# Loading a 2 KB-wide strip of the first tile in three transfers (112, 8 and 8 rows) instead of one of 128 rows

## The chip, the cores and the metric

The kernel runs on one core of one Trainium2 chip. The metric is device time in microseconds (us) per execution; the kernel before takes 121.96 us, the median of three runs that lie between 121.9 and 121.97. All other times in this document are from one profiled execution, and are counted from the first instruction in its span.

## The reference

The input is 32 x 3 images of 256 x 256 float32, 25.17 MB. Each image is turned by 180 degrees:

```python
def reference(x):                                   # x: (32, 3, 256, 256) float32
    return np.rot90(x, k=2, axes=(-2, -1)).astype(np.float32)
```

Turning an image by 180 degrees reverses the order of its 65,536 numbers. No arithmetic is done on them: the work is 25.17 MB read from device memory (HBM), 25.17 MB written back, and a reversal between the two.

## The kernel before

The 96 images are taken in three groups of 32. An image is cut in four parts of 16,384 numbers, and a group then has 32 x 4 = 128 rows of 16,384 numbers (64 KB), one for each partition of the on-chip memory. Three tiles, `A`, `Bt` and `Ct`, hold the three groups; all three fit at the same time, so no tile is used twice and nothing waits for a buffer to come free. A small tile `T` of 2,048 columns is scratch.

For a group there are three steps:

1. *Load* (`load`, line 49): the 128 rows are copied from `x` into the tile. The loads of `Bt` and `Ct` are one transfer each, issued by the SP engine's queue. The load of `A` is two transfers: columns 512 to 16,383 through SP (line 62), and the strip of columns 0 to 511, 2 KB of each row, through the queue of the ACT engine (line 63). ACT has no other work in this kernel.
2. *Turn* (`turn` and `swap`, lines 54 to 71): VectorE (DVE) reverses every row in place. A piece of width `w` is swapped with the piece at the mirrored place in three copies: the high end reversed into `T`, the low end reversed to the high end, and `T` to the low end. All three are recorded at line 44. `A` and `Ct` are turned in four pieces of 2,048 columns (12 copies), `Bt` in six pieces of up to 1,366 (18 copies).
3. *Store* (`store`, line 52): the tile is written to `out`, the four parts of each image in reverse order. All three stores go through SP's queue.

The order on each queue follows the program text. SP issues: load `A` (columns from 512), load `Bt`, load `Ct`, store `A`, store `Bt`, store `Ct`. DVE does all of `A`, then all of `Bt`, then all of `Ct`, in program order, because `copy` asks for that order. Two waits matter below. The first copy of `A` (`T<-A`) reads the last 2,048 columns of the tile, so it waits for SP's transfer alone; the second (`A<-A`) reads columns 0 to 2,047, which hold the strip, so it is the one that waits for ACT's transfer. And the store of `A` has a manual dependency (lines 75 to 79) on the last copy of `Bt`: SP doesn't issue the first store before DVE has turned both `A` and `Bt`, and the two stores behind it on SP wait with it.

Of the kernel before, what the change touches and what calls it, by code (L numbers as in the profile page):

```python
# [2 lines left out]

os.environ.setdefault("NEURON_RT_ULTRASERVER_MODE", "4")

# [4 lines left out]


@with_exitstack
def kernel(
    ctx: ExitStack,
    tc: tile.TileContext,
    x: bass.AP,
    out: bass.AP,
):
    nc = tc.nc  # L20
    P = 128

    B, C, H, W = x.shape
    L = H * W
    G = 32
    E = L // 4
    J = E // 8

    x4 = x.rearrange("b c h w -> (b c) (h w)").rearrange(
        "(g n) (s e) -> g (n s) e", n=G, s=4)  # L30
    o4 = out.rearrange("b c h w -> (b c) (h w)").rearrange(
        "(g n) (s e) -> g n s e", n=G, s=4)

    pool = ctx.enter_context(tc.tile_pool(name="slots", bufs=1))
    A = pool.tile([P, E], x.dtype, tag="A")
    Bt = pool.tile([P, E], x.dtype, tag="B")
    Ct = pool.tile([P, E], x.dtype, tag="C")
    T = pool.tile([P, J], x.dtype, tag="T")

    def back(t, lo, hi):  # L40
        return t[:, hi - 1:(lo - 1 if lo else None):-1]

    def copy(dst, src):
        c = nc.vector.tensor_copy(out=dst, in_=src)  # L44
        tc.keep_in_program_order(c)
        return c

    def load(t, g, lo=0, hi=E, queue=nc.sync):
        return queue.dma_start(out=t[:, lo:hi], in_=x4[g][:, lo:hi])  # L49

    def store(t, g):
        return nc.sync.dma_start(out=o4[g][:, ::-1, :], in_=t[:, :])

    def swap(t, lo, w):
        hi = E - lo - w
        copy(T[:, 0:w], back(t, hi, hi + w))
        copy(t[:, hi:hi + w], back(t, lo, lo + w))
        return copy(t[:, lo:lo + w], T[:, 0:w])

    half = E // 2  # L60

    load(A, 0, 512, E)
    load(A, 0, 0, 512, nc.scalar)
    load(Bt, 1)
    load(Ct, 2)

    def turn(t, pieces):
        step = -(-half // pieces)
        for lo in range(0, half, step):
            last = swap(t, lo, min(step, half - lo))  # L70
        return last

    turn(A, 4)
    last = turn(Bt, 6)
    tc.add_manual_dep(
        store(A, 0).ins, last.ins.name,
        mybir.DependencyInfo(
            mybir.DependencyClass.Sync, mybir.DependencyReason.DATA),
        reason="the first store goes when the loads are nearly done")
    store(Bt, 1)  # L80
    turn(Ct, 4)
    store(Ct, 2)


# [1 line left out]
_INS = ['x']  # L86
_OUTS = [((32, 3, 256, 256), 'float32')]


# [23 lines left out]
```

## Time and profile before

| What | us |
|---|---|
| median of the three timed runs | 121.96 |
| span of the profiled execution (first to last instruction) | 120.1 |
| DVE busy | 45.2, in 42 copies |
| one DVE copy of 2,048 / 1,366 columns | 1.23 / 0.87 |
| SP's load of `A`, issue to landing | 21.9 |
| ACT's strip, issue to landing | 22.1 |
| load of `Bt` / of `Ct`, issue to landing | 40.8 / 59.7 |
| store of `A` / of `Bt` / of `Ct`, issue to landing | 22.2 / 40.9 / 42.7 |

The page gives no time for the profiled execution except its span; the timed runs lie 1.9 us above that span. A transfer's time to landing counts from its issue and includes its time behind earlier transfers in the same queue. Bytes are moved by 16 DMA engines; a transfer's rows are dealt out to them. In the trace each record of a DMA engine is called a packet. Here a packet is one row of one transfer, or the 4-byte write with which a DMA engine reports on a semaphore that its share of a transfer is done. SP's queue is q1 in the records, ACT's is q10.

### The profile page before, as it was taken

The numbers are of one execution on the slowest core, as the hardware profiler recorded it, in microseconds if no ns is written. First come the engines' busy times: TensorE is split into PE (matmuls) and PEld (weight loads), VectorE is DVE, ScalarE is ACT, GpSimd is POOL, SyncE is SP. The second block draws the span as 40 slices with busy tenths as digits, with TensorE's granted clock in tenths as the row PEclk, the third lists the DMA queues.
The fourth block names the chain that finished last, engine by engine and source line by source line (L and its number), as shares of the span: only waits on it lengthen the run. The fifth ranks groups of instructions, "written<-read, shape, count | busy, mean of one in ns | idle before, by whom it ended". The sixth has DMA issues, their size and how long they took to land.

```text
span 120.1 us, 99 instructions
## 1 busy us (share of the span) xinstructions
DVE 45.2 (38%) x42; POOL 0.2 (0%) x4
## 2 busy tenths in 40 slices
DVE  0000000499995099999459999400000000000000
POOL 0000000000000000000000000000000000000000
DMA  9888988899889988998899889988898889888980
GB/s 338 349 349 349 699 349 349 360 633 415 349 349 589 459 349 349 568 480 349 349 502 546 349 349 458 589 349 349 349 699 349 349 349 699 349 349 349 677 371 0
DMA packets 1008, 50.33 MB, mean 419 GB/s; under 512 B 112, under 2 KB 112, under 8 KB 240
## 3 DMA queue, kind: packets, MB, share of 16 engines
q1 hardware_dynamic: 864, 50.07, 96.9%
q10 hardware_dynamic: 144, 0.26, 0.6%
HBM read 25.17 MB, written 25.17 MB: 419 GB/s over the span
## 4 chain that ended last, share of the span: by engine, by line
DMA 34%; DVE 26%; another core or an unknown queue 2%; issue 1%; SPq 0%; DVEq 0%
DMA Bt<-in_x_dram 34%; DVE Bt L44 9%; DVE T L44 9%; DVE Ct L44 8%; SPq L49 0%; DVEq L44 0%
## 5 line engine op out<-in xcount | busy, mean ns | idle before, releaser
L44 DVE COPY T<-A 128x2048 f32<-128x2048 f32 x4 | 4.9, 1227 | 22.8 <-DMA A<-in_x_dram 22.7
L44 DVE COPY T<-Bt 128x1366 f32<-128x1366 f32 (+1 forms) x6 | 5.2, 873 | 4.5 <-DMA Bt<-in_x_dram 4.3
L44 DVE COPY T<-Ct 128x2048 f32<-128x2048 f32 x4 | 4.9, 1227 | 3.2 <-DMA Ct<-in_x_dram 3.1
L44 DVE COPY Bt<-T 128x1366 f32<-128x1366 f32 (+1 forms) x6 | 5.2, 873 | 0.2
L44 DVE COPY Bt<-Bt 128x1366 f32<-128x1366 f32 (+1 forms) x6 | 5.2, 872 | 0.2
L44 DVE COPY Ct<-T 128x2048 f32<-128x2048 f32 x4 | 4.9, 1227 | 0.1
L44 DVE COPY A<-T 128x2048 f32<-128x2048 f32 x4 | 4.9, 1227 | 0.1
L44 DVE COPY Ct<-Ct 128x2048 f32<-128x2048 f32 x4 | 4.9, 1227 | 0.1
L44 DVE COPY A<-A 128x2048 f32<-128x2048 f32 x4 | 4.9, 1226 | 0.1
L97 POOL MEMSET const-bfloat16-1.0<- 128x1 bf16 x1 | 0.1, 102 | 0.0
L97 POOL MEMSET const-uint8-127<- 128x1 uint8 x1 | 0.1, 102 | 0.0
L97 POOL MEMSET const-float32-0.0<- 128x1 f32 x1 | 0.1, 98 | 0.2 <-issue 0.2
L97 POOL MEMSET const-float32-1.0<- 128x1 f32 x1 | 0.1, 98 | 0.0
## 6 DMA issues: line engine op xcount, KB each, us to landing
A<-in_x_dram SPq DMA_DIRECT2D x1, 7936.0 KB, 21.9
A<-in_x_dram ACTq DMA_DIRECT2D x1, 256.0 KB, 22.1
Bt<-in_x_dram SPq DMA_DIRECT2D x1, 40.8
Ct<-in_x_dram SPq DMA_DIRECT2D x1, 59.7
out_dram<-A SPq DMA_DIRECT2D x1, 22.2
out_dram<-Bt SPq DMA_DIRECT2D x1, 40.9
out_dram<-Ct SPq DMA_DIRECT2D x1, 42.7
```

The source lines that it names most:

```text
L44: c = nc.vector.tensor_copy(out=dst, in_=src)
L97: nc = _bacc.Bacc("TRN2", target_bir_lowering=False, num_devices=1)
```

## The change

The strip of `A` is still loaded through ACT's queue, and every element goes where it went. The one transfer of 128 rows becomes three transfers: rows 0 to 111, rows 112 to 119, rows 120 to 127. ACT issues them one after the other. Each has its own semaphore, so the second copy of `A` (`A<-A`), which waited for one strip transfer, waits for three; so does the store of `A`, which in the kernel before lists the strip's semaphore among its waits too. Everything else, the order on SP's queue and on DVE included, is as it was.

```diff
     load(A, 0, 512, E)
-    load(A, 0, 0, 512, nc.scalar)
+    for r0, r1 in ((0, 112), (112, 120), (120, 128)):
+        nc.scalar.dma_start(out=A[r0:r1, 0:512], in_=x4[0][r0:r1, 0:512])
     load(Bt, 1)
     load(Ct, 2)
```

## The prediction, made before the changed kernel ran

> **What bounds the kernel now.** I read the page's DMA part first, because DVE is busy for only 38% of the span.
>
> ```profile
> DMA  9888988899889988998899889988898889888980
> ...
> q1 hardware_dynamic: 864, 50.07, 96.9%
> q10 hardware_dynamic: 144, 0.26, 0.6%
> ...
> A<-in_x_dram SPq DMA_DIRECT2D x1, 7936.0 KB, 21.9
> A<-in_x_dram ACTq DMA_DIRECT2D x1, 256.0 KB, 22.1
> ```
>
> The DMA engines are busy from start to end: 96.9% + 0.6% of all 16. The kernel is bound by bytes, and its time changes only if a DMA engine gets more to do or falls idle. The last two lines show something else: 256 KB through ACT took as long as 7,936 KB through SP. The packet records tell why. They carry no engine number, but each begins within some nanoseconds of another's end, so they fall into 16 chains, one for each DMA engine. This is the chain whose eighth row of `A` ends last (start us, queue, bytes, ns):
>
> ```
> 17.393 q1  63488 2342
> 19.732 q10  2048   84
> 19.812 q1  63488 2342
> 22.150 q10  2048   84
> 22.230 q1      4    9
> 22.236 q10     4    9
> 22.242 q1  65536 2418
> 24.656 q1  65536 2418
> ```
>
> A DMA engine takes the two queues in turn, one packet from each: a row from SP, a strip row from ACT, and so on. The 4-byte completion writes take turns too (SP's stood between the last strip row and the strip's own). So a strip row costs 0.08 us of the DMA engine but waits one SP row, 2.34 to 2.42 us, for its turn. Eight strip rows beside eight rows of `A` finish together, at 22.2.
>
> Next the timeline, to see what stands between the loads and the stores:
>
> ```profile
> 0.73 0.38 ACTq L49 DMA_DIRECT2D A<-in_x_dram  x1
> 0.73 0.39 SPq L49 DMA_DIRECT2D A<-in_x_dram  x1
> ...
> 22.69 1.23 DVE L44 COPY T<-A 128x2048 f32<-128x2048 f32 x1 [22.69 <-DMA A<-in_x_dram]
> 23.95 1.23 DVE L44 COPY A<-A 128x2048 f32<-128x2048 f32 x1
> ...
> 36.56 1.23 DVE L44 COPY A<-T 128x2048 f32<-128x2048 f32 x1
> 42.11 0.87 DVE L44 COPY T<-Bt 128x1366 f32<-128x1366 f32 x1 [4.32 <-DMA Bt<-in_x_dram]
> ...
> 57.53 0.87 DVE L44 COPY Bt<-T 128x1362 f32<-128x1362 f32 x1
> 58.43 0.63 SPq L52 DMA_DIRECT2D out_dram<-A  x1
> 59.10 0.59 SPq L52 DMA_DIRECT2D out_dram<-Bt  x1
> 61.45 1.23 DVE L44 COPY T<-Ct 128x2048 f32<-128x2048 f32 x1 [3.05 <-DMA Ct<-in_x_dram]
> ```
>
> `A` is turned by 37.79, then DVE waits 4.32 us for `Bt`; `Bt` is turned by 58.40, and SP issues the first store at once. The waits of SP confirm that the store waited for DVE and nothing else at the end:
>
> ```profile
> SPq L52 <- DVE Bt L44: 35.5, 1, 35.5
> ```
>
> By the packet records the rows of `Ct`'s load end at 60.46 to 60.88 on the 16 DMA engines, and each takes its first store row 2 to 5 ns later. The store was issued 2.0 to 2.4 us ahead. That lead, and the 4.32 us before `Bt`, is all the slack DVE has.
>
> **The change part by part.**
>
> *More issues on ACT.* Two further issues of about 0.38 us (the row at 0.73) put the last at about 1.6 us. ACT has nothing else to do, and the strip rows are first needed at 21.8: nothing, bounded by 0 and by the 20 us of that cover.
>
> *Bytes per DMA engine.* 128 rows were 8 on each chain. 112 rows over 16 are 7 each; the two transfers of 8 rows have no example in the trace. I take one row each on eight DMA engines (the shown transfers deal equal numbers of whole rows); the other end, all eight rows on one DMA engine, is a rival below. If both use the same eight, these get 9 strip rows and 3 completion writes: +0.08 + 2 x 0.006 = +0.09 us; the others get 7: -0.08 us. The DMA engine that ends last sets the end, and which group it is in isn't recorded: -0.08 to +0.09, I take 0. On that spread the Trainium skill ("DMA: Bandwidth & Descriptors", section "Why a DMA increments its semaphore by 16 and not by 1") says that a transfer uses the largest number up to 16 that divides its rows, the lowest-numbered DMA engines first, so 8 and the same 8; no run here shows it yet.
>
> *Turns.* On a DMA engine of the eight, ACT's queue now holds seven rows, completion 1, a row, completion 2, a row, completion 3: 12 packets instead of 9. Played on the chain above, with SP's eighth row of `A` ending at t: completion 1, SP's own completion, second strip row, a row of `Bt` (2.41), completion 2, a row of `Bt` (2.41), third strip row, a row of `Bt` (2.41), completion 3. That is t + 3 x 2.414 + 2 x 0.08 + 2 x 0.006 = t + 7.42. t is 21.71 to 22.15 on the 16 chains, at least 21.90 for the latest of any eight, so the last completion is at 29.32 to 29.57. From record to landing it is 0.42 (SP's load of `A`) to 0.62 (the strip: 22.24 to 22.86): 29.74 to 30.2. I take 30.1, since the strip's own row is the nearest.
>
> *The second copy.* `A<-A` starts at 30.1 instead of 23.95. Behind it on DVE stand ten more copies of `A`, 13.84 us to 37.79 before. They now end at 43.94 and eat the 4.32 us of waiting: `Bt`'s first copy starts at 43.97, not 42.11, 1.86 us later (1.5 to 1.95 by the range above). Its 18 copies take the same 16.29 us, so SP issues the first store at 60.29 (59.93 to 60.38) instead of 58.43. `Ct` lands at 61.36, so its turn isn't late. The store of `Bt`, queued behind on SP, is hidden by the 19 us of `A`'s rows.
>
> *The gap between loads and stores.* The only transfer in the trace that meets idle DMA engines is the first load: issued at 0.73, first packets at 1.756 to 2.086 (1.03 to 1.36 later), ends of these at 4.777 to 5.222, so 3.0 to 3.4 us for what later takes 2.34. The store then begins at 60.29 + 1.03 to 1.36 = 61.32 to 61.65 on DMA engines that are idle since 60.4 to 60.9. Their first store rows ended at 63.30 at the latest. Without any cold start, the last now ends at 61.65 + 2.42 = 64.07: +0.77. With the load's cold start, 60.29 + 4.49 + 0.08 = 64.86: +1.56, or +1.80 if the store's longer issue (0.63 beside 0.39) counts as well. The 23 rows behind it run as before, so this is the change of the end. I take +1.25, about midway: a store reads on-chip memory, and the cold row is a load's. With the early and late ends of the issue the bounds are +0.4 and +1.9.
>
> Sum: span 120.1 + 1.25 = 121.3; with the 1.9 us by which the timed median lies above the profiled span, 123.2 us.
>
> **The rivals.**
>
> *Hidden after all (not slower).* If fewer turns are needed, say because a completion write and the row behind it go in one turn, the strip lands one or two turns earlier, at 27.7 or 25.2. DVE's slip of 6.15 us becomes 3.7 or less and the 4.32 us before `Bt` cover it. The point that decides: the free slip is 42.11 - 37.82 = 4.29 us, and about 1.0 us more, since a store issued at 59.5 still reaches the DMA engines by 60.88. Landings up to 29.2 cost nothing; my figure is 0.5 to 1.0 beyond that. Time: 121.96 - 0.08 to + 0.09, so 121.9 to 122.05. Against it: every 4-byte write in the records took a turn of its own. The Trainium skill speaks for it ("DMA: Bandwidth & Descriptors", section "Queues, rings and completion order"): a DMA engine takes a whole packet from one queue, typically 9 to 17 descriptors, before it switches, by which ACT's remaining packets would go together and this rival would hold; the trace's strict alternation of single rows disagrees. Chance 0.14.
>
> *More turns.* The 8-row transfers lie on fewer DMA engines. On four, two rows each: two more turns, landing at 35.1, store issued 5 us later still, 128 us; on one, some 13 turns more, above 150. One turn more for a reason that I don't see: 125.7. Chance together 0.10.
>
> *Better balance (faster).* The DMA engines end at 118.45 to 118.94. If the late ones all lose a row and the strip stays hidden, -0.08 us; a gain above 0.24 needs a mechanism that no row shows. Chance 0.02.
>
> **How the numbers follow.** The forecast, a gap of 0.4 to 1.9 us (122.3 to 123.9), has 0.74, likeliest 123.2. The range takes in the hidden case below and a little above the forecast's own range: 121.9 to 124.1; it leaves out the more-turns case and tails. A measurement here tells 0.2%, 0.24 us, from no change. Slower by more: 0.70 of the forecast (a gap that just closes takes 0.04 from it) and 0.10, so 0.80; same 0.18 (the hidden case and those 0.04); faster 0.02.
>
> The Trainium skill advises against such splits altogether ("DMA: Bandwidth & Descriptors", section "Rules for kernel authors": one 128-partition transfer, since parts run on the same DMA engines); it names no price.
>
> **What would show it.** In the profile after: 160 packets in q10 (128 rows, 16 + 8 + 8 completions); the third strip transfer landing at about 30; idle time of some 6.1 us before the second copy of `A` with a DMA as its end; no wait before `Bt`; the first store issued near 60.3; a slice of lower DMA share near 61; each later landing about 1.2 us later. The prediction is wrong if `A<-A` starts before 29.2, if the store's rows begin less than 1 us after its issue, or if the strip lands near 35 or later.

## The result and the profile after

The changed kernel takes 123.47 us (median of four runs, 123.46 to 123.73) where the kernel before takes 121.94: a ratio of 1.0131 (95% interval 1.0117 to 1.0146), 1.5 us slower. The forecast was 123.2, in a range of 121.9 to 124.1.

These are the same parts of the page as before, now of the changed kernel: the DMA engines' busy tenths in 40 slices, the queues, and the DMA issues with their time to landing.

```profile
span 121.9 us, 103 instructions
...
DMA  9778998899778977897787977797779777977990
...
q1 hardware_dynamic: 864, 50.07, 96.2%
q10 hardware_dynamic: 160, 0.26, 0.6%
...
A<-in_x_dram SPq DMA_DIRECT2D x1, 7936.0 KB, 23.0
A<-in_x_dram ACTq DMA_DIRECT2D x1, 224.0 KB, 22.8
A<-in_x_dram ACTq DMA_DIRECT2D x2, 16.0 KB
...
Ct<-in_x_dram SPq DMA_DIRECT2D x1, 60.8
```

ACT's queue has 160 packets, 16 completions more than before. But two lines say something that was not foreseen: SP's load of `A` takes 23.0 us to land instead of 21.9, and that of `Ct` 60.8 instead of 59.7. The loads themselves became slower. Next the timeline of the changed kernel around the waits (start, duration, engine, line; in brackets the idle time before it and what ended it):

```profile
0.73 1.32 ACTq L64 DMA_DIRECT2D A<-in_x_dram  x3
...
23.74 1.23 DVE L44 COPY T<-A 128x2048 f32<-128x2048 f32 x1 [23.74 <-DMA A<-in_x_dram]
31.05 1.23 DVE L44 COPY A<-A 128x2048 f32<-128x2048 f32 x1 [6.08 <-DMA A<-in_x_dram]
...
43.66 1.23 DVE L44 COPY A<-T 128x2048 f32<-128x2048 f32 x1
44.92 0.87 DVE L44 COPY T<-Bt 128x1366 f32<-128x1366 f32 x1
...
61.24 0.62 SPq L52 DMA_DIRECT2D out_dram<-A  x1
...
62.52 1.23 DVE L44 COPY T<-Ct 128x2048 f32<-128x2048 f32 x1 [1.31 <-DMA Ct<-in_x_dram]
```

The new wait of 6.08 us stands before the second copy of `A`, the wait before `Bt` is gone, and the first store is issued at 61.24 instead of 58.43. A slice of lower DMA share near 61 us, which the forecast looked for, does not stand out in the DMA row, since the whole row is lower than before. The packet records give the gap: the last rows of `Ct` end at 61.40 to 61.92 on the 16 DMA engines, their first store rows begin together at 62.51 to 62.66. From the last end to the last beginning it is 0.74 us of idle time.

In this profile, of an execution that took 123.73 us, the end of the last store row is 1.87 us later than before (120.80 beside 118.93): 1.04 had accumulated when the last row of `Ct` ended (61.92 beside 60.88), and the rest arose at the gap and behind it. So the loss has two parts, of which one was not in the prediction's sum. The experiments separate them.

### The profile page after: what moved, and what is told of

It is laid out like the page before. It is cut to its first block, busy times and chain, and to the rows that moved or that the text cites. A ratio compares the mean times of both kernels' runs of the same rounds, so it can differ in the third digit from the quotient of the medians.

```text
span 121.9 us, 103 instructions
## 1 busy us (share of the span) xinstructions
DVE 45.2 (37%) x42; POOL 0.2 (0%) x4
## 4 chain that ended last, share of the span: by engine, by line
DVE 36%; DMA 24%; another core or an unknown queue 1%; issue 1%; ACTq 1%; DVEq 0%
DMA A<-in_x_dram 24%; DVE T L44 11%; DVE Bt L44 9%; DVE A L44 8%; DVE Ct L44 8%; ACTq L64 1%; DVEq L44 0%
## 6 DMA issues: line engine op xcount, KB each, us to landing
Ct<-in_x_dram SPq DMA_DIRECT2D x1, 60.8
```

## The experiments

Three theories stood against each other. *W*: the late strip makes DVE late, hence the first store, hence the DMA engines fall idle (the prediction's). *L*: three transfers slow the loads. *U*: the uneven shares (nine strip rows on eight DMA engines, seven on the others) are at fault. When L had proved right in part, it was split further, into *S* (each additional transfer or packet has a price) and *P* (a strip row slows others when a DMA engine writes it to partitions that another one is writing).

### The changed kernel once more

> The changed kernel once more, unaltered. In its first profile the end came 1.87 us later than before, of which 0.8 us arose at the gap between the last row of the load of Ct (61.92) and the first store rows (62.51 to 62.66), and 1.04 us earlier: rows of A between about 9 and 22 us took 2.42 to 2.66 us where before all took 2.34. Theory L (the three transfers themselves slow the loads): the slow rows are there again, A lands near 23.7, the time is 123.4 to 123.7. Theory C (chance of that execution): rows of A take 2.34 us again, A lands at 22.6 to 22.9, the first store is issued near 60.3 and the last landing is about 0.9 us later than before; a time of 122.9.

123.51 us, ratio 1.0134 (1.0118 to 1.015). `A` lands at 23.24 (0.73 + 22.5), between the figures of the two theories, `Ct` at 62.06 instead of 61.36, and the last store row ends 1.56 us later than before. The lateness of the loads is there again, 0.70 us; the additional 0.3 of the first profile was that execution's own. Theory C falls.

### Three even transfers: 96, 16 and 16 rows

```diff
-    for r0, r1 in ((0, 112), (112, 120), (120, 128)):
+    for r0, r1 in ((0, 96), (96, 112), (112, 128)):
```

> Also three strip transfers, but of 96, 16 and 16 rows, so that each DMA engine gets 8 strip rows (6, 1, 1) and 11 packets of ACT. Theory W (the late strip makes DVE, the first store and so the DMA engines wait): played by turns, the third completion goes after two rows of Bt instead of three, landing at 27.7; the slip of DVE is 3.7 us, the 4.3 us of waiting before Bt cover it, the first store goes at 58.4 and the time is 121.9 to 122.0. Theory N (three transfers cost as such, whatever DVE does): as the changed kernel, 123.4. If the loads alone are slowed by the number of transfers: 122.3 to 122.9.

122.89 us, ratio 1.0076 (1.0058 to 1.0094). The timeline of this variant:

```profile
29.05 1.23 DVE L44 COPY A<-A 128x2048 f32<-128x2048 f32 x1 [4.08 <-DMA A<-in_x_dram]
43.53 0.87 DVE L44 COPY T<-Bt 128x1366 f32<-128x1366 f32 x1 [0.64 <-DMA Bt<-in_x_dram]
59.85 0.63 SPq L52 DMA_DIRECT2D out_dram<-A  x1
62.89 1.23 DVE L44 COPY T<-Ct 128x2048 f32<-128x2048 f32 x1 [3.06 <-DMA Ct<-in_x_dram]
```

With two turns instead of three, DVE waits 4.08 us for the strip and still 0.64 for `Bt`: the slip is covered, as W has it, and the store rows follow those of `Ct` without a gap. The strip landed at 28.93, later than the 27.7 counted for it. Still 0.94 us are lost, where W alone had nothing, and with even shares: U doesn't explain it, L does.

### Four even transfers

```diff
-    for r0, r1 in ((0, 112), (112, 120), (120, 128)):
+    for r0, r1 in ((0, 80), (80, 96), (96, 112), (112, 128)):
```

> Four strip transfers, 80, 16, 16 and 16 rows: every DMA engine gets 8 strip rows (5, 1, 1, 1) and 12 packets of ACT, as many as the eight busier ones have in the changed kernel, but the bytes are even. Theory W: third-row turn as there, landing near 30.1, the first store near 60.3 or a little later with the loads, time 122.9 to 123.6, as the changed kernel. Theory U (the uneven shares, 9 strip rows on eight DMA engines and 7 on the others, make the loss): 121.9 to 122.0.

124.25 us, ratio 1.0174 (1.0153 to 1.0196). The last completion lands at 30.76 and the first store is issued at 61.08, with a gap behind the loads again. As many turns as in the changed kernel, and at least as large a loss without any imbalance: U is out. The time lies 0.65 above the range given; the profiled execution was the shortest of the five (123.64), so why the others take longer isn't seen.

### The strip used last

```diff
-    def turn(t, pieces):
+    def turn(t, pieces, inside_out=False):
         step = -(-half // pieces)
-        for lo in range(0, half, step):
+        los = list(range(0, half, step))
+        for lo in los[::-1] if inside_out else los:
...
-    turn(A, 4)
+    turn(A, 4, inside_out=True)
```

> The changed kernel with its three transfers as they are, but A is turned from the inside out: the piece that reads the strip comes fourth instead of first. Its A<-A then would start at about 35.3 and the strip, landing at 30 to 31, is not waited for. Theory W: no wait for the strip, A turned by 37.8 to 38.9, DVE waits for Bt again, the first store is issued 2 us ahead of the loads' end, no gap; 121.9 to 122.0 if the loads are not slowed by the three transfers, 122.3 to 123.0 if they are (theory L). If DVE's wait isn't the cause: 123.4.

122.63 us, ratio 1.0059 (1.0045 to 1.0074). The same three transfers, but nothing waits for them:

```profile
43.09 0.87 DVE L44 COPY T<-Bt 128x1366 f32<-128x1366 f32 x1 [4.43 <-DMA Bt<-in_x_dram]
59.42 0.63 SPq L52 DMA_DIRECT2D out_dram<-A  x1
```

The wait before `Bt` is back at 4.43 us and the gap is gone. It takes 0.88 us less than the changed kernel beside it, which is the price of the gap; 0.68 us remain, which is the price of the slower loads.

### No manual dependency

```diff
     turn(A, 4)
-    last = turn(Bt, 6)
-    tc.add_manual_dep(
-        store(A, 0).ins, last.ins.name,
...
+    store(A, 0)
+    turn(Bt, 6)
```

> The changed kernel without the manual dependency: the store of A is issued after A is turned (near 45), and lines up on SP's queue behind the load of Ct. The late strip remains, but no gap can arise. Theory L (three transfers slow the loads by 0.65 to 0.75 us, apart from the gap): as the variant turned from the inside out, 122.5 to 122.8. If that variant's 122.6 came from its other order of copies: 121.95 here.

122.69 us, ratio 1.0062 (1.0042 to 1.0082). The other way of closing the gap, with the store issued at 44.50 and DVE still waiting 6.04 us for the strip, gives the same. So the remaining loss doesn't depend on the order of the copies.

```profile
30.64 1.23 DVE L44 COPY A<-A 128x2048 f32<-128x2048 f32 x1 [6.04 <-DMA A<-in_x_dram]
```

### The gap alone

```diff
+    for _ in range(5):
+        copy(T[:, 0:J], back(A, E - J, E))
     turn(A, 4)
```

> The kernel before, with its one strip transfer, and five more copies of 2,048 columns into the scratch tile ahead of turning A (their result is overwritten; nothing else changes). That makes DVE late by 5 x 1.26 = 6.3 us without touching a transfer. Theory G (the gap between loads and stores has its price by itself, and the slower loads are a second, separate loss): rows of A take 2.34 us as before, A lands at 22.7, the first store is issued near 60.4, its rows begin about 1.3 us later, idle DMA engines for 0.7 to 1.0 us; time 122.7 to 122.95, that is 0.8 to 1.0 more than before and less than the changed kernel. If the gap explains all of the loss: 123.4. If a late store costs nothing: 121.95.

123.38 us, ratio 1.0122 (1.0107 to 1.0137). Here the transfers are those of the kernel before, and `Ct` lands at 61.38 as there; the store is issued late:

```profile
span 121.2 us, 104 instructions
...
22.71 7.53 DVE L44 COPY T<-A 128x2048 f32<-128x2048 f32 x6 [22.71 <-DMA A<-in_x_dram]
60.47 0.63 SPq L52 DMA_DIRECT2D out_dram<-A  x1
61.48 1.23 DVE L44 COPY T<-Ct 128x2048 f32<-128x2048 f32 x1 [1.03 <-DMA Ct<-in_x_dram]
```

The last row of `Ct` ends at 60.98 (0.10 later than before), the first store rows begin at 61.75 to 61.90 (0.92 from the last end to the last beginning), take 2.47 instead of 2.42 us, and the rows behind them lose another 0.1 in sum: the last store row ends 1.13 us later than before, and the span is 1.1 longer. This shows the gap as a cause by itself. The time, though, grew by 1.48, above the range given and equal to the 123.4 of the theory that the gap explains all of the loss. That theory is out by the two variants above, which lose 0.68 and 0.79 us without a gap. Of the 1.48, the span shows 1.1; 2.2 us lie outside the span in all four executions, where the kernel before, run beside it, and the other variants have 1.8. Where those 0.4 us come from stays open; the five additional instructions are the only other difference.

### Two transfers of all rows, half as wide

```diff
-    load(A, 0, 0, 512, nc.scalar)
+    load(A, 0, 0, 256, nc.scalar)
+    load(A, 0, 256, 512, nc.scalar)
```

together with the removal of the manual dependency as above, on the kernel before.

> The strip in two transfers of all 128 rows, 256 columns each, so that each DMA engine writes strip rows to the same partitions as its rows of A, as before; 18 packets of ACT on every DMA engine. They land late, near 44, so the store of A has no manual dependency here and everything DVE does stays covered. Theory P (strip rows slow the loads when a DMA engine writes them to partitions that another DMA engine is writing at full rate): rows of A take 2.34 us plus nothing, the time is 121.9 to 122.1. Theory S (more strip transfers or packets on ACT's queue slow the loads as such): slow rows of A and Bt, at least as many as with three transfers, 122.5 or more.

122.98 us, ratio 1.0085 (1.007 to 1.01), a time that speaks for S; but the trace does not. With 288 packets ACT's queue has more than in any other variant, and yet every row of `A` behind the first takes 2.342 us, every row of `Bt` 2.418 us, as before. All of the loss is in the last rows of `Ct`, which began at 58.14 to 58.59 and took 2.94 to 3.79 us instead of 2.42. The first store had been issued at 56.33, earlier than in the kernel before (58.43) and later than in the variant without the manual dependency (44.50):

```profile
56.33 0.63 SPq L52 DMA_DIRECT2D out_dram<-A  x1
```

That was tested apart, with `turn` returning the last copy of its first piece:

```diff
-    turn(A, 4)
-    store(A, 0)
-    turn(Bt, 6)
+    turn(A, 4)
+    first = turn(Bt, 6)
+    tc.add_manual_dep(
+        store(A, 0).ins, first.ins.name,
...
```

> The two transfers of 128 rows by 256 columns once more, with the first store issued near 59 (after the first piece of Bt) instead of at 56.3. In the first of the two all rows of A and of the loads up to 58 took their normal time, and the 0.86 us that were lost arose in the last rows of the load of Ct, beginning 1.8 us after the store was issued. If the time of the store's issue did that: no slow rows at all here, 121.9 to 122.1. If the strip transfers did it, whatever the store: the last rows of Ct slow again, 122.9 to 123.1.

121.99 us, ratio 1.0003 (0.9994 to 1.0013). The timeline shows the same late strip (18.80 us of waiting) and the store now issued at 58.93:

```profile
span 120.1 us, 102 instructions
...
42.34 1.23 DVE L44 COPY A<-A 128x2048 f32<-128x2048 f32 x1 [18.80 <-DMA A<-in_x_dram]
58.93 0.63 SPq L52 DMA_DIRECT2D out_dram<-A  x1
```

No slow rows of `Ct`, no loss. So the 0.86 us went with the moment of the store's issue, and 18 strip packets on each DMA engine cost nothing measurable: S falls. (Six of the 256 rows of `Bt` and `Ct` took 0.04 to 0.2 us more in this profile, and none but the last rows of `Ct` in the one before it; that stays unexplained.)

### Which rows go together: halves, and even and odd rows

Both variants have two transfers of 64 rows, 4 + 4 rows and two completions on each DMA engine. First the halves:

```diff
-    for r0, r1 in ((0, 112), (112, 120), (120, 128)):
+    for r0, r1 in ((0, 64), (64, 128)):
```

> The strip in two transfers of 64 rows (0 to 63, 64 to 127): 4 + 4 rows and two completions on every DMA engine, landing near 25.3, covered by DVE's slack. Theory P: rows land on other DMA engines than with one transfer of 128, so rows of A take more than 2.34 us by some 0.04 to 0.09 us each; if half of the rows stay with their DMA engine 122.1 to 122.35, if nearly none do 122.45 to 122.7. Theory S (transfers as such): one more transfer than before, a loss of about 0.3, 122.2 to 122.3. Neither: 121.95.

122.65 us, ratio 1.006 (1.0041 to 1.008). Then the even and the odd rows:

```diff
-    for r0, r1 in ((0, 112), (112, 120), (120, 128)):
-        nc.scalar.dma_start(out=A[r0:r1, 0:512], in_=x4[0][r0:r1, 0:512])
+    for r in (0, 1):
+        nc.scalar.dma_start(out=A[r::2, 0:512], in_=x4[0][r::2, 0:512])
```

> The strip in two transfers of 64 rows like the variant in halves (122.65), but even rows and odd rows instead of the lower and the upper half; 4 + 4 rows on every DMA engine, landing near 27. Theory P needs to know which partitions a DMA engine has in a 128-row transfer. If it has eight neighbours (0 to 7, 8 to 15, ...), the even and the odd rows of a DMA engine are its own: no slow rows, 121.9 to 122.0. If it has two blocks of four (0 to 3 and 32 to 35, ...), most rows fall on others: slow rows as with the halves or more, 122.5 to 122.8. Theory S (number of transfers): 122.65, as the halves.

121.90 us, ratio 0.9997 (0.9988 to 1.0007). The two differ in which rows a transfer covers, in the tile and so also in the input; the next section takes up the input. Their timelines, halves first:

```profile
23.08 1.23 DVE L44 COPY T<-A 128x2048 f32<-128x2048 f32 x1 [23.08 <-DMA A<-in_x_dram]
28.23 1.23 DVE L44 COPY A<-A 128x2048 f32<-128x2048 f32 x1 [3.92 <-DMA A<-in_x_dram]
59.02 0.62 SPq L52 DMA_DIRECT2D out_dram<-A  x1
```

```profile
22.65 1.23 DVE L44 COPY T<-A 128x2048 f32<-128x2048 f32 x1 [22.65 <-DMA A<-in_x_dram]
27.77 1.23 DVE L44 COPY A<-A 128x2048 f32<-128x2048 f32 x1 [3.90 <-DMA A<-in_x_dram]
58.57 0.63 SPq L52 DMA_DIRECT2D out_dram<-A  x1
```

With the same wait for the strip, `A` lands 0.43 us later with the halves. The strip lands a turn later than I had counted for the halves (28.1, not 25.3): in both variants ACT's first row goes after SP's second row instead of its first.

The packet records show the difference row by row. This is the mean time in ns of SP's rows of 62 and 64 KB, over all 16 DMA engines (in groups of 16 by their start), rows 2 to 8 of `A` and 1 to 3 of `Bt`:

```
                        A2   A3   A4   A5   A6   A7   A8   B1   B2   B3
before                2342 2342 2342 2342 2342 2342 2342 2418 2418 2418
changed, first        2342 2353 2647 2453 2421 2435 2444 2573 2423 2580
changed, again        2342 2342 2399 2447 2389 2411 2427 2545 2421 2578
halves                2346 2342 2386 2449 2432 2345 2413 2601 2515 2424
even and odd rows     2344 2342 2342 2342 2342 2342 2342 2418 2418 2418
256 columns, twice    2342 2342 2342 2342 2342 2342 2342 2418 2418 2418
```

In the changed kernel the rows from A4 on take some 0.05 to 0.1 us more (A4 of the first profile 0.3), B1 and B3 some 0.15, and B2, which has only completion writes of ACT beside it, takes its normal time. A strip row itself takes 0.084 us. So the loss is where strip rows are, and whether there is one depends on which rows go together. That is the pattern of P. Its cause, that the slow variants write strip rows by other DMA engines than the rows of `A` of the same partitions, is inferred and not shown: the records name neither DMA engines nor partitions. The expectation tied 121.9 to DMA engines that have eight neighbouring partitions each; the time doesn't show that either, since it isn't recorded how the rows of a transfer with a step are dealt out. And P doesn't say why the first one or two strip rows cost almost nothing: they run beside A2 and A3 too, and those take their normal time.

### Which side: other source rows

```diff
-    load(A, 0, 0, 512, nc.scalar)
+    nc.scalar.dma_start(out=A[:, 0:512], in_=rows[56:184, 0:512])   # rows: x as 384 rows of 16,384
```

> The kernel before with one strip transfer of 128 rows, whose rows are read 56 rows further on in the input (rows 56 to 183 instead of 0 to 127) and are written to the same partitions as before. The strip therefore holds other data than the reference asks for; all transfers have the same size and order. Theory P with the on-chip side as its place (a DMA engine that writes strip rows to partitions which another DMA engine writes at full rate): nothing changes, rows of A take 2.34 us, 121.9 to 122.0. Theory P with the HBM side as its place (a strip row read from where another DMA engine reads): rows of A take more, 122.4 to 122.7.

121.99 us, ratio 1.0003 (0.9993 to 1.0013), and all rows of `A` behind the first take 2.342 us. The strip then holds other numbers, but is written as before. Reading strip rows from elsewhere in HBM costs nothing here, which leaves the writing side as the likely place of the loss.

### A strip twice as wide

```diff
-    load(A, 0, 512, E)
+    load(A, 0, 1024, E)
     for r0, r1 in ((0, 112), (112, 120), (120, 128)):
-        nc.scalar.dma_start(out=A[r0:r1, 0:512], in_=x4[0][r0:r1, 0:512])
+        nc.scalar.dma_start(out=A[r0:r1, 0:1024], in_=x4[0][r0:r1, 0:1024])
```

on the variant without the manual dependency.

> The changed kernel without the manual dependency (122.69), with a strip twice as wide: 1,024 columns in transfers of 112, 8 and 8 rows; same number of transfers and packets, 4 KB in a strip row. Theory P: a strip row takes another DMA engine's partitions for twice the time, slow rows lose about 0.16 instead of 0.08 us, the loss of 0.7 doubles: 123.1 to 123.5. Theory S (packets or transfers have a price, not bytes): 122.5 to 122.8.

123.87 us, ratio 1.0162 (1.0134 to 1.019). The load of `Ct` lands at 64.0 instead of 62.2 (in a profile of the longest execution, 124.43). The loss grows with the bytes and not with the number of packets, as P says, but by more than P's estimate: 2.0 us where 1.4 were expected from twice 0.7, above the range given. In B1 and B3 of that long execution the extra time was 0.42 us instead of about 0.15. So the loss is not simply the strip row's own time; by what rule it grows is open.

## Why the prediction was right, and where it was not

**The direction and the mechanism were right, and the runs show it.** The turns are as played: on eight of the 16 chains ACT's packets go strip row, completion, a row of `Bt` and so on, with three rows of `Bt` before the third completion. This is such a chain of the changed kernel (start us, queue, bytes, ns), from SP's last row of `A` on:

```
20.308 q1  63488 2431
22.735 q10     4    9
22.741 q1      4    9
22.747 q10  2048   99
22.841 q1  65536 2548
25.386 q10     4    9
25.392 q1  65536 2418
27.806 q10  2048  111
27.907 q1  65536 2551
30.454 q10     4    9
```

From the end of SP's row to the third completion it is 7.72 us, where 7.42 was worked out; the 0.3 are the slow rows. The wait before the second copy of `A` was to be some 6.1 us and is 6.08 and 6.23 in the two profiles. The copy itself starts at 31.05 instead of 30.1, because SP's last row of `A` ended 0.6 us later on this chain and the turns took 0.3 longer. The rivals fell with this. A completion and the row behind it do not share a turn, so the strip was not hidden; the Trainium skill's rule that would have hidden it ("DMA: Bandwidth & Descriptors", section "Queues, rings and completion order": a packet of typically 9 to 17 descriptors before a switch) does not hold for these rows. Nor were there more turns: eight DMA engines have nine strip rows and eight have seven, as the forecast took it. The semaphore of the second transfer has one record at 1.83 and eight at 25.43 to 25.86. Here the trace agrees with the Trainium skill ("DMA: Bandwidth & Descriptors", section "Why a DMA increments its semaphore by 16 and not by 1"): a transfer of 8 rows uses 8 DMA engines, and the rest of the count is written at once.

**The step that failed is "bytes per DMA engine".** It was put at -0.08 to +0.09 us and taken as 0, because it counted only the time that a strip row takes of its own DMA engine. The measured price is 0.68 and 0.79 us in the two variants of the same three transfers without a gap. What the runs show in place of the term is that SP's rows beside strip rows take longer in some cuts of the strip and not in others, and that strip rows can take longer too (99 and 111 ns in the chain above instead of 84). The likely reason is that cutting the 128 rows at 112 moves most strip rows to other DMA engines than those that load the same partitions through SP. If so, the trace of before could not show it, since with one transfer of 128 rows the two never cross. The Trainium skill has both halves of it ("SBUF — State Buffer", section "SBUF: two separate sides": DMA ports can be contended for when several DMA engines write to them; and "DMA: Bandwidth & Descriptors", section "The descriptor swizzle": in a transfer to 128 partitions each DMA engine writes one port). The runs fit this, in that one way of cutting the strip into 64 + 64 rows slows SP's rows and another doesn't; a port itself no run shows, nor which partitions a DMA engine has.

**The step "the gap between loads and stores" was too dear.** It was taken as 1.25, between 0.77 and 1.80. Of its parts, the first store rows begin 1.27 to 1.42 us after the issue (1.03 to 1.36 was taken from the load), and the cold start, put at some 0.5, is 0.055 us: the first store rows take 2.47 us instead of 2.42. The issue itself came as far ahead of the loads' end as worked out (0.68 us instead of 0.59), because both moved by about 1 us. So the 0.77 of the case without a cold start was nearly right: the gap is 0.74 us in the first profile, and 0.055 and about 0.1 us in the rows behind it come on top. The gap's price is 0.88 us by the time of the changed kernel against that with the strip used last. The run with the gap alone lost more, 1.1 us in its span, since its loads were not late and its gap was 0.92 us wide.

**So the total came out near for the wrong split.** 1.25 + 0 was forecast; measured are about 0.85 for the gap and 0.7 for the loads, together 1.5. The two errors, some -0.4 and +0.7, have opposite signs and largely cancel; that the total lies only 0.3 us from the forecast is luck.

## What to carry to other kernels

In all these traces a small transfer beside a large one on another queue advances by one packet for each packet of the large one, and every completion write takes such a turn: to know when it lands, count packets, not bytes. How a transfer beside a saturating load is cut can matter as much as into how many parts: even and odd rows cost nothing here, two halves 0.6%, and two cuts by columns nothing either, though these landed only at 42 us and needed the store's issue moved. And look for a delay's price where its slack ends: the 4.3 us that DVE waited before `Bt` were free, and only the part that made the next transfer's issue too late had a price.

## What the runs showed of the hardware that was not expected

- In the cuts at rows 112 and 120, and at 64, a strip row of 2 KB goes with 62 KB rows that are mostly 0.05 to 0.1 us longer and 64 KB rows that are 0.1 to 0.2 us longer; a strip row of 4 KB went with 64 KB rows 0.42 us longer. With one transfer of all rows, with even and odd rows, or with other source rows, it is 0.
- A store that meets idle DMA engines has hardly any cold start (0.055 us), while the first load's first rows take 0.6 to 1.1 us more than later ones in the kernel before.
- With the store of `A` issued at 56.33, the last rows of `Ct` took 0.86 us longer on the mean; issued at 44.50 or 58.93 there was no such loss. The runs show that it hangs on the moment of the issue, and not why.
- After a gap the store rows behind it lose about 0.1 us in sum, beside runs without a gap.
